# All queries, keys and values projected in the state space stage and kept as rows in DRAM, on one Trainium2 core

## Chip, cores, metric

One core of one Trainium2 chip runs the whole program. The metric is the device time of one execution in microseconds, as the median of three runs. PE is the matrix engine (TensorE), PEld its weight loads, DVE, ACT and POOL the vector, scalar and GpSimd engines, SP the engine that issues most DMAs.

## What is computed

One hybrid decoder layer on a sequence of 1024 positions, width 1024, float32:

```python
xn = rmsnorm(x, norm1_g)
q, k, v, u = split(xn @ w_in)              # 512 columns each; 8 heads of 64 for q, k, v
q, k = rmsnorm(q, q_norm_g), rmsnorm(k, k_norm_g)          # per head
attn = dilated_attention(q, k, v)          # causal, windows 128/512/2048, dilations 1/4/16, merged
ssm = s5_mixer(u, ...)                     # diagonal complex scan, gelu, then gated: z * sigmoid(z @ glu_w + b)
mix = concat(rmsnorm(attn), rmsnorm(ssm))
x = x + mix @ w_out
return x + square(relu(rmsnorm(x, norm2_g) @ w_mlp_up)) @ w_mlp_down
```

## The kernel before

Every large product is done in three passes (`mm3`: high by high, high by low, low by high), with both operands split into a high and a low part by one ACT and one DVE instruction (`split`, `split_scaled`; a weight is split when it is loaded, by `load_w`). The program runs through five stages.

**x and u.** `first_x(t)` loads tile t of the transposed input (128 positions), splits it, writes it to DRAM (`d_x`), takes its mean square (ACT squares; three halving additions, on DVE for even t and on POOL for odd t; one PE product `psn` with a column of ones) and projects the 512 columns of u (`psu`, 24 matmuls of 512 columns). The splits of odd tiles are on POOL.

**State space.** `ssm_tables`, `u_turn` and `ssm_main` make, for four groups of channels, tables (`ec`, `bj`, `bt`), input products (`psb`), a scan (`bw`, the state `X`), output products (`psy`) and the gelu; the last step transposes z (`pszt`) and writes `d_hz`. One of the four complex table products (`ec<-apow`) and two of the four multiplications that form X are on POOL. A written string of steps (u, T, B, t, m, p) sets the order; a "p" advances the projection of the first pair of heads.

**Attention.** Heads are handled in four pairs. `qkv(p)` projects the 384 columns of q, k, v of pair p, tile by tile (`psq`, 24 matmuls of 384 columns for each of 8 tiles): it reads the split x back through the POOL queue (`xt<-d_x`, 1 MB), norms q and k (four ACT squares with a sum, three POOL instructions, one DVE multiply, one ACT copy), transposes them (`pst`) into Qd and K2, and writes V2. `attn(p)` forms scores (`pss`, L541), masks and takes the minimum on DVE (L543), exponentials on ACT (L546), scales on POOL (L549), transposes (`psp`, L564), splits, and weighs the values (`pso`, L575). `weave(a, b, na, nb)` emits two generators in turn so that their shares advance evenly: attn(0), attn(1), attn(2) each beside the projection of the next pair, attn(3) beside `glu` (the gated unit) and `out_ssm` (the state space half of the output product, first 512 columns only).

**Output product.** For each of 8 tiles `out_tile` adds three parts (`out_part`, 12 matmuls each: state space half of columns 512 to 1023, attention half of both column halves), norms and transposes the result, and `operands` makes seven split operands for the last stage, three of them with POOL.

**MLP.** `up_proj` and `down_proj`, block products of 512 columns; not touched.

Tiles of the same place wait for each other: raw loads have two buffers (`rawp`), split weights five (`wp`), PSUM banks `mm` two, `tr` two, `s` three. The framework's scheduler moves instructions a little within an engine; each engine and each DMA queue then runs its own list strictly in order.

Of the kernel before, what the change touches and what calls it, by code (L numbers as in the profile page):

```python
# [8 lines left out]
F32 = mybir.dt.float32  # L9
# [25 lines left out]
def hybrid_layer_kernel(ctx: ExitStack, tc: tile.TileContext, io: dict, out: bass.AP):  # L35
# [27 lines left out]
    d_x = [dram.tile([128, 2, 8, 128], F32, name=f"d_x{t}") for t in range(8)]  # L63
# [34 lines left out]

    def load_rows(name, src, c, gains):

        return [load_w(f"{name}{i}", src[:, 2 * i:2 * i + 2, :], 2, c, gains, 2 * i) for i in range(4)]
# [54 lines left out]
    def kv_tiles(p):  # L156
        k, v, q0, q1 = (6, 7, 8, 9) if p % 2 else (2, 3, 4, 5)
# [3 lines left out]
    wu, kept = [], {}  # L161
    SQ = 170
    XS = 170
    XN = 128
    CA = 1

    def first_x(t):
# [3 lines left out]
        xt = place((2, 3, 4, 5, 2, 3, 0, 1)[t], [128, 2, 1024], F32R, "xt")  # L171
        split(xt[:, 0], xt[:, 1], raw, POOL if XS >> t & 1 else DVE)
# [6 lines left out]
        POOL.dma_start(out=d_x[t].rearrange("p a k m -> p a (k m)"), in_=xt.bitcast(F32))  # L179
        sq = sp2.tile([128, 1024], F32, tag="D", name="sq")  # L180
        if XN >> t & 1:
            nc.sync.dma_start(out=sq, in_=io["x"][t * 128:(t + 1) * 128, :])
            ms = sp2.tile([128, 1], F32, tag="ms", name="ms")
            ACT.activation(sq, sq, AF.Square, accum_out=ms)
        else:
            ACT.activation(sq, raw, AF.Square)
            for n in (512, 256, 128):
                (POOL if SQ >> t & 1 else DVE).tensor_tensor(sq[:, :n], sq[:, :n], sq[:, n:2 * n], op=OP.add)
        if not XN >> t & 1:
            pn = tr_bank("psn")  # L190
            PE.matmul(pn[:, 0:1], lhsT=sq[:, :128], rhs=ones, start=True, stop=True)
            ms = sp2.tile([128, 1], F32, tag="ms", name="ms")
            DVE.tensor_copy(ms, pn[:, 0:1])
# [4 lines left out]
        xv = xt.rearrange("p a (k m) -> p a k m", k=8)  # L198
        for k in range(8):
            mm3(ps, xv[:, 0, k], xv[:, 1, k], wu[k // 2][:, 0, k % 2], wu[k // 2][:, 1, k % 2], k == 0, k == 7)  # L200
        us = sp2.tile([128, 512], F32, tag="qkv_t", name="us")
        ACT.activation(us, ps, AF.Copy, scale=r)
        nc.scalar.dma_start(out=d_u[t * 128:(t + 1) * 128, :], in_=us)
        if t > 5:
            kept[t] = xt
# [122 lines left out]
    def ssm_tables(q):  # L328
# [22 lines left out]
        cmul(POOL if CA else DVE, ca[:, 0], ca[:, 1], a_r, a_i, c_r, c_ni, v1, v2, conj=True)  # L351
# [8 lines left out]
        bt = sp.tile([128, 2, 4, 128], F32, tag="bt", name="bt", bufs=3)  # L360
# [28 lines left out]
    def ssm_main(q, u, Et, ca, bt):  # L389
# [34 lines left out]
        POOL.tensor_tensor(v2, e_i, w_i, op=OP.mult)  # L424
# [3 lines left out]
        POOL.tensor_tensor(v2, e_i, w_r, op=OP.mult)  # L428
# [37 lines left out]
    def qkv(p, small, res):  # L466
        w = load_rows(f"wq{p}_", io["w_qkv"][p], 384, g1)
        K2, Qd, V2 = kv_tiles(p)
        res.update(K2=K2, Qd=Qd, V2=V2)

        def turn(t, qd):
            pt = tr_bank("pst").rearrange("p (h m) -> p h m", h=4)
            for h in range(4):
                PE.transpose(pt[:, h], qd[:, h].rearrange("p a e -> p (a e)"), ident)
            tt = slice(t * 128, (t + 1) * 128)
            split_scaled(Qd[0][:, :, tt], Qd[1][:, :, tt], pt[:, 0:2], gqk[:, 0:1])
            ACT.activation(K2[:, :, tt], pt[:, 2:4], AF.Copy, scale=gqk[:, 1:2])
            DVE.scalar_tensor_tensor(K2[64:128, :, tt], pt[64:128, 2:4], gqk[64:128, 1:2],
                                     K2[64:128, :, tt].bitcast(F32), op0=OP.mult, op1=OP.subtract)
# [611 lines left out]
```

## Time and profile before

| | |
|---|---|
| median of 3 runs | 1213.45 us (1211.04 to 1215.29) |
| the profiled execution | 1220.95 us, of which span 1219.2 us |
[...]
| PE busy | 1139.4 us (93%) |
| DVE busy | 841.0 us (69%) |
| ACT busy, POOL busy | 598.6 us (49%), 354.8 us (29%) |

The span is the time from the first to the last instruction of the profiled execution. A share of busy time is a mean over the five stages; the rows below give it by stage.

### The profile page before, as it was taken

The numbers are of one execution on the slowest core, as the hardware profiler recorded it, in microseconds if no ns is written. First come the engines' busy times: TensorE is split into PE (matmuls) and PEld (weight loads), VectorE is DVE, ScalarE is ACT, GpSimd is POOL, SyncE is SP. The second block draws the span as 40 slices with busy tenths as digits, with TensorE's granted clock in tenths as the row PEclk, the third lists the DMA queues.
The fourth block names the chain that finished last, engine by engine and source line by source line (L and its number), as shares of the span: only waits on it lengthen the run. The fifth ranks groups of instructions, "written<-read, shape, count | busy, mean of one in ns | idle before, by whom it ended". The sixth has DMA issues, their size and how long they took to land.

```text
span 1219.2 us, 16630 instructions
## 1 busy us (share of the span) xinstructions
PE 1139.4 (93%) x5734; PEld 956.7 (78%) x5734; DVE 841.0 (69%) x1557; ACT 598.6 (49%) x1276; POOL 354.8 (29%) x528
## 2 busy tenths in 40 slices
PE   6766989999999999999999999999999999999998
PEld 4554777888898877787777888888878888888887
DVE  7999785567676777666876566665656775576763
ACT  5222233677776786533555555555544333333332
POOL 6685642354545445313312111122110000000000
PEclk9886887899999999999999999999999999999999
DMA  7734432635355425753244434434379999575930
GB/s 288 272 115 106 151 112 70 211 114 178 129 155 170 143 96 166 243 191 121 75 159 173 167 145 165 145 140 167 144 294 398 387 387 352 193 240 183 333 140 35
DMA packets 101093, 227.15 MB, mean 186 GB/s; under 512 B 8848, under 2 KB 27792, under 8 KB 96144
## 3 DMA queue, kind: packets, MB, share of 16 engines
q1 hardware_dynamic: 85136, 154.13, 37.2%
q0 software_dynamic: 14432, 69.22, 15.7%
q10 hardware_dynamic: 1440, 2.73, 0.6%
q8 instruction: 45, 0.74, 0.3%
q14 instruction: 40, 0.33, 0.1%
HBM read 168.93 MB, written 57.11 MB: 185 GB/s over the span
## 4 chain that ended last, share of the span: by engine, by line
PE 70%; DVE 11%; DMA 6%; issue 5%; POOL 4%; ACT 4%; SPq 0%; ACTq 0%; DVEq 0%; POOLq 0%
PE psx L105 7%; PE psx L106 7%; PE psx L107 7%; PE psy L105 7%; PE psy L106 7%; PE psy L107 7%; PE pso L575 3%; PE psq L107 2%; PE psq L105 2%; PE psq L106 2%; PE pss L541 2%; PE psp L564 2%; PE psy L438 1%; PE pso L107 1%; PE pso L105 1%
## 5 line engine op out<-in xcount | busy, mean ns | idle before, releaser
L77 ACT ACTIVATE ud<-raw 128x1024 fp32r<-128x1024 f32 x112 | 112.9, 1053 | 184.8 <-PE psy L107 81.0
L78 DVE TENSOR_TENSOR ud<-raw,ud 128x1024 fp32r<-128x1024 f32 x112 | 132.6, 1221 | 83.6 <-ACT ud L77 83.6
L105 PE MATMUL psx<-X,wu 128*128 128x512 f32 (+1 forms) x260 | 101.1, 389 | 4.5 <-ACT st L871 3.2
L106 PE MATMUL psx<-X,wu 128*128 128x512 f32 (+1 forms) x260 | 100.4, 386 | 0.7 <-DVE X L78 0.7
L107 PE MATMUL psx<-X,wu 128*128 128x512 f32 (+1 forms) x260 | 100.5, 386 | 0.5 <-DVE wu L78 0.5
L105 PE MATMUL psy<-ud 128*128 128x512 f32 x256 | 99.6, 389 | 0.0
L106 PE MATMUL psy<-ud 128*128 128x512 f32 x256 | 99.6, 389 | 0.0
L107 PE MATMUL psy<-ud 128*128 128x512 f32 x256 | 99.6, 389 | 0.0
L78 DVE TENSOR_TENSOR wu<-wm,wu 128x512 fp32r<-128x512 f32 x112 | 75.5, 701 | 30.8 <-ACT wu L77 30.6
L105 PE MATMUL psq<-wq,xt 128*128 128x384 f32 x256 | 93.7, 366 | 0.9 <-DMA xt<-d_x 0.8
L77 ACT ACTIVATE wu<-wm 128x512 fp32r<-128x512 f32 x112 | 66.7, 625 | 53.1 <-DMA wm<-in_w_up_dram 27.0
L106 PE MATMUL psq<-wq,xt 128*128 128x384 f32 x256 | 90.6, 354 | 0.5 <-DVE wq L82 0.5
L107 PE MATMUL psq<-wq,xt 128*128 128x384 f32 x256 | 90.8, 355 | 0.0
L875 POOL DMA_DIRECT2D d_a<-st x80 | 43.5, 544 | 130.1 <-DVE st L884 65.9
L106 PE MATMUL psx<-ud 128*128 128x512 f32 x192 | 74.8, 390 | 0.0
L105 PE MATMUL psx<-ud 128*128 128x512 f32 x192 | 74.7, 389 | 0.0
L107 PE MATMUL psx<-ud 128*128 128x512 f32 x192 | 74.7, 389 | 0.0
L980 DVE TENSOR_TENSOR raw<-raw 128x1024 f32<-128x1024 f32 x40 | 49.7, 1249 | 28.7 <-DMA raw<-in_w_down_dram 28.7
L549 POOL TENSOR_SCALAR s<-s,dn 128x128 f32<-128x128 f32 (+3 forms) x64 | 50.2, 787 | 47.9 <-DVE dn L548 45.9
L78 DVE TENSOR_TENSOR pt<-psp,pt 128x128 fp32r<-128x128 f32 (+2 forms) x96 | 51.1, 552 | 15.9 <-ACT pt L77 15.2
L105 PEld LDWEIGHTS psx<-X,wu 128*128 128x128 f32 x260 | 48.8, 188 | 16.5 <-ACT st L871 4.6
L575 PE MATMUL pso<-pt,V 128*128 128x256 f32 x320 | 54.6, 294 | 3.5 <-ACT pt L77 1.9
(294 smaller groups left out, 3012.5 us busy)
## 6 DMA issues: line engine op xcount, KB each, us to landing
raw<-in_w_down_dram SPq DMA_DIRECT2D x96, 512.0 KB, 9.0
xt<-d_x POOLq DMA_DIRECT2D x30, 1024.0 KB, 5.2
raw<-d_a SPq DMA_DIRECT2D x56, 512.0 KB, 8.1
d_a<-st POOLq DMA_DIRECT2D x80, 256.0 KB, 2.6
wm<-in_w_up_dram SPq DMA_DIRECT2D x32, 512.0 KB, 3.7
d_x<-xt POOLq DMA_DIRECT2D x8, 1024.0 KB, 5.1
d_a<-o POOLq DMA_DIRECT2D x32, 256.0 KB, 2.8
wq_r<-in_w_qkv_dram SPq DMA_DIRECT2D x16, 384.0 KB, 3.9
```

Of the source, the lines that this page charges most:

```text
L77: ACT.activation(h, src, AF.Copy)
L78: eng.tensor_tensor(l, src, h.bitcast(F32), op=OP.subtract)
L105: PE.matmul(ps, lhsT=ah, rhs=bh, start=start, stop=False, skip_group_check=more)
L106: PE.matmul(ps, lhsT=ah, rhs=bl, start=False, stop=False, skip_group_check=more)
L107: PE.matmul(ps, lhsT=al, rhs=bh, start=False, stop=stop, skip_group_check=more)
L438: PE.matmul(psy[s][:, a], lhsT=X[s * 64:s * 64 + 64, ri, a, :], rhs=ca[s * 64:s * 64 + 64, ri, a].rearrange("p d c -> p (d c)"), start=Fal ...
L541: PE.matmul(ps[:, :cw], lhsT=Qd[a][:, h, b * 128:(b + 1) * 128], rhs=K2[:, h, c0:c0 + cw], start=a == 0, stop=a == 1)
L549: POOL.tensor_scalar(s[:, :n], s[:, :n], dn, 1.0, op0=OP.mult, op1=OP.mult)
L564: PE.transpose(ps[:, kb * 128:(kb + 1) * 128], P[j][:, (k0 + kb) * 128:(k0 + kb + 1) * 128], ident)
L575: PE.matmul(po[:, :256], lhsT=V2[:, k0 + kb, h, :], rhs=pt[:, a, kb, :], start=k0 + kb == 0 and a == 0, stop=k0 + kb == nb - 1 and a == 1)
L875: POOL.dma_start(out=d_a[blk // 2][i][blk % 2], in_=st)
L980: DVE.tensor_tensor(rb, rb, raw_unit(wd(n, *b1)), op=op)
```

## The change

The projection of q, k and v no longer goes by pairs of heads. `project(c)` projects all 512 columns of q (c=0), k (c=1) or v (c=2), 24 matmuls of 512 columns for each of 8 tiles, all in the state space stage; two "p" are one tile. The split x of all tiles stays in SBUF (six places and the two U buffers), so only four tiles are written to `d_x` and read back. q and k are normed there (one ACT square, one DVE reduction, three POOL instructions, one DVE multiply, one POOL copy) and written to DRAM as rows `d_q`, `d_k`; v goes to `d_v`. `heads(p)` later reads the rows of a pair, transposes them four tiles at a time and makes Qd, K2 and V2. The weave partners of the four attentions are now the heads of the next pair and pieces of `glu` and `out_ssm`; `out_ssm` does both column halves, so that `out_tile` has two parts instead of three. The sums for the norms of x, attn and ssm become 8 or 4 PE products with ones instead of additions on DVE or POOL. Everything that `first_x`, `ssm_tables`, `ssm_main` and `operands` gave to POOL as a two-input operation goes to DVE.

```diff
+    ORDER = ((6, 7, 0, 1, 2, 3, 4, 5), (4, 5, 0, 1, 2, 3, 6, 7), (2, 3, 0, 1, 6, 7, 4, 5))
+    BACK = {(1, 6): 4, (1, 7): 5, (2, 4): 2, (2, 5): 3}
-            for n in (512, 256, 128):
-                (POOL if SQ >> t & 1 else DVE).tensor_tensor(sq[:, :n], sq[:, :n], sq[:, n:2 * n], op=OP.add)
...
+        for k in range(8):
+            PE.matmul(pn[:, 0:1], lhsT=sq[:, k * 128:k * 128 + 128], rhs=ones, start=k == 0, stop=k == 7)
...
+    def project(c):
+        w = [load_w(f"wq{c}_{i}", io["w_qkv"][c, :, 2 * i:2 * i + 2, :], 2, 512, g1, 2 * i) for i in range(4)]
+        for t in ORDER[c]:
+            if (c, t) in BACK:
+                res[t] = place(BACK[c, t], [128, 2, 1024], F32R, "xt")
+                POOL.dma_start(out=res[t], in_=d_x[t])
+            ps = mm_bank("psq")
+            x_mm(ps, res[t], w, range(4))
+            yield
+            x_mm(ps, res[t], w, range(4, 8))
+            if c < 2:
+                row = sp2.tile([128, 8, 2, 64], F32, tag="rows", name="rows")
+                sq = row[:, :, 1]
+                ACT.activation(sq, ps.rearrange("p (h e) -> p h e", e=64), AF.Square)
+                f = sp2.tile([128, 8], F32, tag="f", name="f")
+                DVE.tensor_reduce(f, sq, axis=AX.X, op=OP.add)
+                rsqrt(f, f, r2[:, t:t + 1], 8)
+                POOL.tensor_scalar(f, f, rstd1[:, t:t + 1], 1.0, op0=OP.mult, op1=OP.mult)
+                DVE.tensor_tensor(row[:, :, 0], ps.rearrange("p (h e) -> p h e", e=64),
+                                  f[:, :, None].to_broadcast([128, 8, 64]), op=OP.mult)
+                POOL.tensor_scalar(row[:, :, 1], row[:, :, 0], 1.0, 1.0, op0=OP.mult, op1=OP.mult)
...
+            nc.sync.dma_start(out=d_qkv[c][t * 128:(t + 1) * 128, :], in_=row)
...
-        cmul(POOL if CA else DVE, ca[:, 0], ca[:, 1], a_r, a_i, c_r, c_ni, v1, v2, conj=True)
+        cmul(DVE, ca[:, 0], ca[:, 1], a_r, a_i, c_r, c_ni, v1, v2, conj=True)
...
-        POOL.tensor_tensor(v2, e_i, w_r, op=OP.mult)
+        DVE.tensor_tensor(v2, e_i, w_r, op=OP.mult)
...
+    def heads(p, out_):
+        K2, Qd, V2 = kv_tiles(p)
...
+            for c in range(2):
+                st = rawp.tile([128, 1024], F32, tag="raw", name="qk_r").rearrange("p (t h e) -> p t h e", t=4, h=2)
+                rows(c, 4 * hf, 4, st.rearrange("p t h e -> p t (h e)"), 256)
+                for h in range(2):
+                    pt = tr_bank("pst")
+                    for t in range(4):
+                        PE.transpose(pt[:, t * 128:t * 128 + 128], st[:, t, h], ident)
+                    if c == 0:
+                        split_scaled(Qd[0][:, h, tt], Qd[1][:, h, tt], pt, gqk[:, 0:1])
...
-    weave(attn(3, **prev), tail(), 24.5, 43.0)
+    weave(attn(0, **cur[0]), chain(heads(1, cur[1]), some(g, 5)), 24.5, 17.0)
+    weave(attn(1, **cur[1]), chain(heads(2, cur[2]), g, some(o, 2)), 24.5, 17.0)
+    weave(attn(2, **cur[2]), chain(heads(3, cur[3]), some(o, 6)), 24.5, 19.7)
+    weave(attn(3, **cur[3]), o, 24.5, 21.6)
```

Where the instructions stand now, at three places. First PE at the end of the state space stage, before: the last transposes of z (`pszt`) stand among scores of attn(0) (`pss`) and the projection of the second pair (`psq`).

```order
L541 MATMUL pss<-K_944,Qd 128x256 x4
L105 MATMUL psq<-wq_0_2040,xt 128x384
L106 MATMUL psq<-wq_0_2040,xt 128x384
L461 MATMUL pszt<-pack,z_1867 128x128 x8
L107 MATMUL psq<-wq_0_2040,xt 128x384
L105 MATMUL psq<-wq_0_2040,xt 128x384
L474 MATMUL pst<-pack,qd 128x128 x4
```

Now 228 of the 576 `psq` stand behind the last `pszt`, and behind the last of them the transposes of rows (`pst`) and the scores follow directly:

```order
L103 MATMUL psq<-wq_3_2263,xt 128x512
L104 MATMUL psq<-wq_3_2263,xt 128x512
L506 MATMUL pst<-pack,qk_r 128x128 x8
L542 MATMUL pss<-K_2423,Qd 128x256 x6
L506 MATMUL pst<-pack,qk_r 128x128 x12
L542 MATMUL pss<-K_2423,Qd 128x256 x2
L542 MATMUL pss<-K_2423,Qd 128x384 x2
```

So no projection is left beside the first scores. Second, SP at the same place, before: the mask (`bias`) is loaded between weight loads of the second pair.

```order
L463 DMA d_hz<-hz 128x1024
L91 DMA wq_1_r<-in_w_qkv_dram 128x768
L671 DMA bias<-in_bias_dram 128x1024
L91 DMA wq_2_r<-in_w_qkv_dram 128x768
```

Now the mask stands behind the read-back of v, whose second half waits for the last row of v:

```order
L229 DMA d_v<-row 128x512
L496 DMA v_r<-d_v 128x4x128
L496 DMA qk_r<-d_q 128x4x256
L496 DMA v_r<-d_v 128x4x128
L672 DMA bias<-in_bias_dram 128x1024
```

The load of the mask has moved behind a wait for the end of the projections. Third, DVE in a scan of the state space stage, before (the two products that form `s_1581` and `s_1586` are on POOL):

```order
L417 SCALAR_TENSOR_TENSOR bw<-rho,bw 128x128 x7
L423 TENSOR_TENSOR s_1580<-ec,bw 128x4x127
L427 TENSOR_TENSOR s_1585<-ec,bw 128x4x127
L425 TENSOR_TENSOR X<-s_1580,s_1581 128x4x127
L429 TENSOR_TENSOR X<-s_1585,s_1586 128x4x127
```

Now, with those two products on DVE and the norm of a projected tile (`f`, `rows`) between:

```order
L442 SCALAR_TENSOR_TENSOR bw<-rho,bw 128x128 x7
L448 TENSOR_TENSOR s_1402<-ec,bw 128x4x127
L449 TENSOR_TENSOR s_1403<-ec,bw 128x4x127
L452 TENSOR_TENSOR s_1407<-ec,bw 128x4x127
L450 TENSOR_TENSOR X<-s_1402,s_1403 128x4x127
L453 TENSOR_TENSOR s_1408<-ec,bw 128x4x127
L219 TENSOR_REDUCE f<-rows 128x8
L454 TENSOR_TENSOR X<-s_1407,s_1408 128x4x127
L222 TENSOR_TENSOR rows<-psq,f 128x8x64
```

Two products have moved to DVE and two instructions of the projection have joined the chain.

## Rows read from the trace of the kernel before

**Rows 1.** Stages: window, length; busy PE, PEld, DVE, ACT, POOL; clock, DMA share, GB/s.

```profile
0.00:79.00 79.00, 54.99 (x215) 43.16 (x215) 67.80 (x223) 30.05 (x39) 53.23 (x61) 0.92 0.66 240
79.00:226.00 147.00, 119.14 (x770) 100.36 (x771) 111.17 (x195) 47.07 (x139) 74.53 (x91) 0.76 0.38 113
226.00:515.00 289.00, 273.97 (x1683) 244.06 (x1681) 206.50 (x560) 205.87 (x626) 138.15 (x230) 1.00 0.49 161
515.00:597.00 82.00, 78.78 (x362) 64.80 (x361) 55.23 (x81) 33.79 (x72) 23.68 (x33) 0.94 0.45 148
597.00:1219.20 622.20, 612.49 (x2707) 504.35 (x2707) 400.34 (x502) 281.83 (x404) 65.25 (x116) 1.00 0.60 214
```

**Rows 2.** The same windows for tile psq: PE, PEld, DVE, ACT.

```profile
79.00:226.00 147.00, 48.02 (x198) 40.53 (x199) 5.39 (x15) 10.00 (x71) 0.76 0.38 113
226.00:515.00 289.00, 120.80 (x567) 95.60 (x565) 19.14 (x50) 31.66 (x217) 1.00 0.49 161
```

**Rows 3.** Timeline of PE near 266 us: start, duration, instruction.

```profile
265.80 0.33 PE L105 MATMUL psq<-wq,xt 128*128 128x384 f32 x1
265.97 0.33 PE L106 MATMUL psq<-wq,xt 128*128 128x384 f32 x1
```

**Rows 4.** Timeline of PE near 800 us.

```profile
800.50 0.39 PE L105 MATMUL psy<-X,wu 128*128 128x512 f32 x1
800.73 0.39 PE L106 MATMUL psy<-X,wu 128*128 128x512 f32 x1
```

**Rows 5.** Tile psn: instructions, duration min/median/max.

```profile
L520 PE MATMUL psn<-ones,ssq x32: 164/250/352, 461.4 to 558.3; 128*128 128x1 f32 x32
```

**Rows 6.** Timeline of DVE, 102 to 111 us.

```profile
102.04 1.58 DVE L115 TENSOR_TENSOR s<-eh,el 128x512 f32<-128x512 f32 x1
...
109.94 0.68 DVE L114 TENSOR_TENSOR s<-rpow,bb 128x512 f32<-128x512 f32 x1
110.54 0.68 DVE L115 TENSOR_TENSOR s<-rpow,bb 128x512 f32<-128x512 f32 x1
```

**Rows 7.** Timeline of POOL at 103 us.

```profile
103.04 1.54 POOL L115 TENSOR_TENSOR s<-apow,pack 128x512 f32<-128x512 f32 x1
```

**Rows 8.** Groups of DVE by line and shape, 226 to 515 us: busy, mean ns.

```profile
L82 DVE SCALAR_TENSOR_TENSOR wq<-wq_r,pack,wq 128x384 fp32r<-128x384 f32 x18 | 10.6, 614 | 3.6 <-ACT wq L81 3.6
L748 DVE SCALAR_TENSOR_TENSOR x<-pso,rsm,x 128x512 f32<-128x512 f32 x8 | 6.0, 746 | 2.1 <-DMA x<-in_x_dram 2.1
```

**Rows 9.** The stretch 226 to 515 for tile pst: PE, PEld, DVE, ACT.

```profile
226.00:515.00 289.00, 15.57 (x100) 11.36 (x100) 24.82 (x52) 24.11 (x51) 1.00 0.49 161
```

**Rows 10.** The same stretch for attention's lines L541, L564, L575: PE, PEld.

```profile
226.00:515.00 289.00, 47.63 (x188) 30.54 (x188) 1.00 0.49 161
...
226.00:515.00 289.00, 45.39 (x288) 34.00 (x288) 1.00 0.49 161
...
226.00:515.00 289.00, 54.62 (x320) 44.80 (x320) 1.00 0.49 161
```

**Rows 11.** The chain that ended last, at two places: start, duration.

```profile
227.88 5.90 DMA bias<-in_bias_dram
...
268.56 0.87 PE psp L564 x8
```

**Rows 12.** DMA issues by line: size, median us to landing.

```profile
xt<-d_x POOLq DMA_DIRECT2D x30, 1024.0 KB, 5.2
...
d_x<-x SPq DMA_DIRECT2D x24, 256.0 KB, 2.4
```

**Rows 13.** Windows of all engines: two stretches of the state space stage.

```profile
104.00:122.00 18.00, 11.23 (x62) 9.14 (x62) 16.20 (x28) 2.83 (x6) 6.60 (x8) 0.53 0.20 36
200.00:221.00 21.00, 21.00 (x70) 17.11 (x70) 8.82 (x25) 8.34 (x18) 4.08 (x7) 0.51 0.16 54
```

**Rows 14.** Who waited for whom, 226 to 515 us: total, times, longest.

```profile
DVE pt L78 <- ACT pt L77: 15.2, 27, 2.0
```

**Rows 15.** Tile psu: ACT's copy of a tile, duration min/median/max.

```profile
L202 ACT ACTIVATE us<-psu,rstd x8: 667/684/690, 22.0 to 79.3; 128x512 f32<-128x512 f32 x8
```

More of the change, by code (lines that the diff above doesn't have):

```diff
@@ L170, in first_x @@
         nc.sync.dma_start(out=raw, in_=io["x_t"][t])
-        xt = place((2, 3, 4, 5, 2, 3, 0, 1)[t], [128, 2, 1024], F32R, "xt")
-        split(xt[:, 0], xt[:, 1], raw, POOL if XS >> t & 1 else DVE)
+        if t < 6:
+            xt = place(t, [128, 2, 1024], F32R, "xt")
+        else:
+            xt = sp.tile([128, 2, 1024], F32R, tag="U", name="xt", bufs=2)
+        split(xt[:, 0], xt[:, 1], raw)
         if not wu:
@@ L517, in mix_scale, with rows @@
-    def mix_scale(a, tiles):
-        for t in tiles:
-            pn = tr_bank("psn")
-            PE.matmul(pn[:, 0:1], lhsT=ssq[:, a, t * 128:(t + 1) * 128], rhs=ones, start=True, stop=True)
-            vs = part("vs", [128, 1], "vs")
-            DVE.tensor_copy(vs, pn[:, 0:1])
-            rsqrt(rsm[:, t, a:a + 1], vs, 1.0 / 512, 1)
+        out_.update(K2=K2, Qd=Qd, V2=V2)
+        def rows(c, t0, nt, to, w):
+            nc.sync.dma_start(out=to, in_=d_qkv[c][t0 * 128:(t0 + nt) * 128, w * p:w * p + w].rearrange("(t m) c -> m t c", m=128))
@@ L657, in hybrid_layer_kernel @@
             next(main[q], None)
-    assert next(proj, None) is None
+    for n, _ in enumerate(proj):
+        if n == 12:
+            first = heads(0, prev)
+        if n > 12:
+            next(first)
+    for _ in first:
+        pass
     ssm.close()
@@ L730, in operand, with load_mix @@
         return XC[i]
-    def mixed(t, a):
-        return [x[:, t // 2] for x in operand(MIX[t % 2, a])]
-    def load_mix(t, a):
-        mx = rawp.tile([128, 1024], F32, tag="raw", name="mx")[:, :512].rearrange("p (k m) -> p k m", k=4)
-        nc.sync.dma_start(out=mx, in_=d_mix[a][:, :, t * 128:(t + 1) * 128].rearrange("k p m -> p k m"))
-        split(*mixed(t, a), mx)
+    def load_mix(t, a, where):
+        mx = rawp.tile([128, 1024], F32, tag="raw", name="mx")
+        mv, sq = [mx[:, i * 512:i * 512 + 512].rearrange("p (k m) -> p k m", k=4) for i in range(2)]
+        nc.sync.dma_start(out=mv, in_=d_mix[a][:, :, t * 128:(t + 1) * 128].rearrange("k p m -> p k m"))
+        mt = place_turn(where, [128, 2, 4, 128], F32R, "mt")
+        split(mt[:, 0], mt[:, 1], mv)
+        ACT.activation(sq, mv, AF.Square)
+        pn = tr_bank("psn")
+        for k in range(4):
+            PE.matmul(pn[:, 0:1], lhsT=sq[:, k], rhs=ones, start=k == 0, stop=k == 3)
+        vs = part("vs", [128, 1], "vs")
+        DVE.tensor_copy(vs, pn[:, 0:1])
+        rsqrt(rsm[:, t, a:a + 1], vs, 1.0 / 512, 1)
+        return mt
@@ new lines, in some @@
+    def some(gen, n):
+        for _ in range(n):
+            v = next(gen, None)
+            if v is None:
+                return
+            yield v
+    cur = [prev, {}, {}, {}]
+    g, o = glu(), out_ssm()
+    weave(attn(0, **cur[0]), chain(heads(1, cur[1]), some(g, 5)), 24.5, 17.0)
+    weave(attn(1, **cur[1]), chain(heads(2, cur[2]), g, some(o, 2)), 24.5, 17.0)
+    weave(attn(2, **cur[2]), chain(heads(3, cur[3]), some(o, 6)), 24.5, 19.7)
+    weave(attn(3, **cur[3]), o, 24.5, 21.6)
```

216 lines of the change are left out of this document (74 added, 142 removed).

## The prediction, on record before the run

> **What bounds the kernel now.** Read first the windows by stage [rows 1]. In the MLP (622.2 us) PE is busy 612.5, and the change does not touch it. In the attention stage (289 us) PE is busy 274.0 at full clock, a share of 0.948, with DVE and ACT at 206 each: PE sets the pace. In the output product (82 us) PE has 78.8. The state space stage (147 us) is the loose one: PE 119.1 at a mean clock of 0.76, DVE 111.2; neither is full, and the chains between DVE, ACT, POOL and PE set the end. The first stage (79 us) has DVE at 67.8 and PE at 55.0. So the idle PE time is in the first 226 us, and PE work that leaves the attention stage is worth its full time.
>
> **The projections cost PE the same.** Two 384-column matmuls follow each other after 0.17 us [rows 3], two of 512 columns after 0.23 [rows 4]. Before: 768 x 0.174 = 134 us. After: 576 x 0.227 = 131 us. The change saves no projection; it moves it.
>
> **First stage.** 64 products with ones replace 7 single ones; each is two matmul rows, so 128 rows instead of 14. The trace has no long run of them: a lower bound is the 0.87 us for eight 128-column matmuls [rows 11], 0.11 a row, an upper one the median 0.25 [rows 5]; I take 0.11, as these also queue behind one another. That is +12 us of PE in a stage with 24 us of PE idle. DVE gains four splits of 1024 columns and loses twelve halving additions, which I take as nil. 79 stays 79; at worst the 12 us would lie on the path.
>
> **State space stage.** Without `psq` PE has 119.1 - 48.0 = 71 us there [rows 1, 2], 54 of it if the clock were full. All 131 us of projection now come in. By the order of PE 348 of the 576 `psq` (79 us) stand among the state space products and 228 (52 us) behind the last of them. DVE loses `psq` work (5.4) and most of its transposed splits and gains: 32 products from POOL at 0.60 from start to start [rows 6], 19 us; reduction and multiply of about 14 tiles, 28 x 0.6 = 17; six more weights split. Against that stands what POOL costs DVE now: with a two-input POOL product running (1.54 us) [rows 7] the same DVE product takes 1.58 instead of 0.68 [rows 6]. I estimate 15 such collisions (between none and all 32), which gives 13 us back. DVE: 111 - 11 + 19 + 17 + 4 - 13 = 127 us for the mixed part. PE has 133 to 150 there. Both stay under or at the 147 of before, so I take 150 for the mixed part, 52 for the rest at full clock and 3 for the 32 transposes of the first pair: 205, or **+58**. Bounds: +42 (PE never waits and always has full clock: 54 + 131 + 4 = 189) and +96 (all added projection, 131 - 35, serial to the 147).
>
> [...]
>
> Four tiles of x still come back through POOL, 5.2 us each [rows 12]. By the order each is issued at least two tiles (11 us) ahead of its matmuls, so they are hidden; without that cover they would cost up to 21. The rows written and read back are 21 MB in place of some 30 MB of x; the DMA share is 0.38 to 0.49 here [rows 1], no bound. The next matrix's weights are split while PE finishes the tile before, one of four ahead: at most 3 us each time, in the bounds.
>
> **Start of attention.** Before, the mask landed 5.9 us after its issue [rows 11] while PE had projections of the second pair. Now none is left, the mask's load stands on SP behind the read-back of v, and that waits for the last row of v. After the last `psq`: ACT's copy 0.7 [rows 15], the row's write 2.4 [rows 12], the mask 5.9: 9 us, less 1.5 of transposes and scores that PE can do. [...] I add 2.5 for some 5 us of attention's work at half clock: **+10** (bounds 3 and 18).
>
> **Attention.** Of the 567 `psq` that leave the stage, each frees 0.174: 98.7 us. In come 96 matmuls of the second column half of `out_ssm`, 21.8, and 36 rows of `psn`, 4. The transposes stay. PE: 274.0 - 98.7 + 21.8 + 4 = 201 us. DVE: 206.5 less `psq` work 19.1 [rows 2], less weights 10.6 [rows 8], and the Q and K splits fall from 24.8 (52 of 256 columns) [rows 9] to about 17 (24 of 512 at 0.7), with six for V at 0.7, +4, and eight more output additions at 0.75 [rows 8], +6: 179. ACT falls from 206 by at least 31.7 [rows 2], to under 175. POOL loses all norms and sums. PE still has the most to do, but 179 beside 201 is close, where it was 206 beside 274. With PE's share at 0.948 the stage would take 212; at 0.92, which I take since the partners are thinner, 201 / 0.92 = 219: **-70**. Bounds: 212 (-77) and, at a share of 0.79, 254 (-35).
>
> **Output product.** 96 matmuls leave (21.8 us), 59 rows of `psn` come (6.5): PE 78.8 - 15.3 = 63.5, and at 0.91 of the time 70: **-12**. DVE keeps 55 (eight additions less, twelve subtractions from POOL more), a share of 0.79, so it can take back some: bounds -5 and -17.
>
> **Sum.** 58 + 10 - 70 - 12 = **-14**: a span of 1205 instead of 1219.2. The profiled execution took 1220.95, 7.5 above the median; taken from the median 1213.45, the change gives **1199**.
>
> **Rivals.**
> *Attention runs at the pace of its own chain (slower).* In that chain scores go PE, DVE, ACT, DVE, POOL, PE, ACT, DVE, PE. Its own matmuls are 47.6 + 45.4 + 54.6 = 148 us [rows 10]; beside them PE had 126 us of other work to fill waits, and will have 53. Its waits are there now: DVE stands 15.2 us for ACT's half of the split [rows 14], with all that other work beside it; the masking of the next scores is queued behind it on DVE, and PE's next transposes wait for the bank. At a PE share of 0.79 the stage takes 254 and the median comes to 1234. It decides below 0.86: 79 + 205 + 10 + 201 / 0.86 + 70 + 622 = 1219. Against it: at 219 us DVE's share is 0.82 and ACT's under 0.80.
> *The state space stage stretches.* PE is in order, and a projection that waits for a bank (two `mm` banks, shared with `psb`; a bank is free only after ACT, DVE, three POOL instructions and DVE again) holds back the products of the scan. At +85 instead of +58 the median is 1226. For it: PE was at half clock for much of that stage; against it: projections are ready work, and more of it keeps the clock up.
> *Denser.* If every one of the 32 moved products cost DVE a 0.9 us wait before, the mixed part gives back 29 instead of 13, PE alone bounds it, and the stage comes to +45; with the start at +4, attention at its old share (-77) and the output at -15 that is -43, median 1170.
> *Nothing.* The time only moves: attention at 0.87 gives 1212.
>
> **Chances.** Forecast (1183 to 1208) 0.41; denser 0.11; nothing 0.13; attention's chain 0.22; stretched stage 0.13. A change below 0.3% (1210 to 1217) can hardly be told from none here. Faster: 0.41 + 0.11 = 0.52; same 0.13; slower 0.22 + 0.13 = 0.35. The range of 8 in 10 takes in half of the denser case and of both slower ones: 1172 to 1240; the forecast's own is 1183 to 1208.
>
> **What would show it.** Right: the last `pszt` near 229 us, the last `psq` near 281; a PE gap of 6 to 9 us before the first L543 score instruction, ended by the mask; the last `pso<-pt,V` near 514 with PE at 0.9 or more; output product about 70 us; MLP unchanged at 622. DVE's 512-wide products at 0.68 throughout would show the collisions gone. Wrong: `psq` that waits for DVE's multiply (bank), long DVE idle in attention ended by ACT together with PE below 0.86, or a DVE share above 0.9 in either stage.

## The result, and the profile after

The changed kernel takes **1253.41 us** (median of four runs, 1251.47 to 1257.78) against 1213.45: a ratio of **1.034** (95% interval 1.030 to 1.037). It is 40 us slower; the forecast was 1199, 14 us faster, with a range of 1172 to 1240. The profiled execution took 1253.21 us, its span 1251.4.

The windows of the changed kernel by stage, columns as in [rows 1] (first stage; the part where projections stand among the state space products; the tail of projections alone; the start of attention; attention; output product; MLP):

```profile
0.00:75.00 75.00, 65.86 (x375) 55.83 (x376) 55.36 (x228) 33.08 (x42) 31.03 (x41) 1.00 0.59 205
75.00:247.00 172.00, 139.04 (x834) 109.19 (x833) 111.52 (x218) 36.79 (x58) 60.27 (x83) 0.87 0.34 110
247.00:308.00 61.00, 58.23 (x258) 47.35 (x257) 11.54 (x16) 15.46 (x22) 10.12 (x16) 0.94 0.47 156
308.00:326.00 18.00, 10.36 (x53) 8.50 (x51) 9.21 (x27) 9.67 (x23) 2.44 (x6) 0.72 0.72 233
326.00:563.00 237.00, 210.40 (x1208) 173.37 (x1208) 178.19 (x454) 148.79 (x317) 64.28 (x104) 0.94 0.36 116
563.00:632.00 69.00, 61.26 (x324) 49.91 (x323) 50.08 (x85) 34.52 (x76) 15.80 (x32) 0.99 0.53 175
632.00:1251.40 619.40, 611.78 (x2712) 505.81 (x2710) 400.44 (x506) 282.25 (x405) 60.56 (x112) 1.00 0.60 214
```

Beside the stages of [rows 1] and the forecast for each:

| stage | before | forecast | after | miss |
|---|---|---|---|---|
| first | 79 | 79 | 75 | -4 |
| state space, all projections | 147 | 205 | 233 | +28 |
| start of attention and attention | 289 | 229 | 255 | +26 |
| output product | 82 | 70 | 69 | -1 |
| MLP | 622.2 | 622.2 | 619.4 | -3 |

Together the miss is 46 us of span. The other 8 of the 54 are the step from the profiled execution to the median: 7.5 us were taken off because the profiled execution before was that far above its median. After, profiled time and median agree.

So two stages went wrong, by nearly the same amount. Look first at the state space stage. In its mixed part neither PE (139 of 172 us) nor DVE (111.5) is full. Who waited for whom there, the first rows for DVE in 75 to 247 us (total, times, longest), then the first for PE in 75 to 308 us:

```profile
DVE rows L222 <- POOL f L221: 28.8, 13, 4.1
DVE f L219 <- ACT rows L217: 10.1, 6, 2.9
...
PE psb L424 <- DVE rows L222: 17.9, 5, 5.0
```

And one such wait in the timeline of PE, ACT, DVE and POOL near 100 us (in square brackets the idle time before, and what ended it):

```profile
98.81 0.39 PE L104 MATMUL psq<-wq,xt 128*128 128x512 f32 x1
...
99.24 0.60 ACT L217 ACTIVATE rows<-psq 128x512 f32<-128x512 f32 x1 [4.50 <-PE psq L104]
...
99.86 0.69 DVE L219 TENSOR_REDUCE f<-rows 128x8 f32<-128x512 f32 x1 [2.90 <-ACT rows L217]
...
100.65 0.27 POOL L74 TENSOR_SCALAR rsq<-f,r 128x8 f32<-128x8 f32 x1 [4.20 <-DVE f L219]
101.01 1.65 POOL L75 TENSOR_TENSOR f<-rsq,mhalf 128x8 f32<-128x8 f32 x1
102.76 0.28 POOL L221 TENSOR_SCALAR f<-f,rstd 128x8 f32<-128x8 f32 x1
...
103.08 0.69 DVE L222 TENSOR_TENSOR rows<-psq,f 128x512 f32<-128x512 f32 x1 [2.53 <-POOL f L221]
...
103.83 1.55 PE L424 MATMUL psb<-U,bt 128*64 128x128 f32 x12 [4.62 <-DVE rows L222]
```

Read it from the bottom: PE's next work, `psb` of the scan, wants an `mm` bank. That bank holds a projected tile until its norm is through: ACT's square, DVE's sum, three POOL instructions, DVE's multiply, 4.5 us from 99.24 to 103.77. Meanwhile DVE does nothing else either: it stands 2.53 us for POOL's factor, and with that the scan behind it in DVE's list. (The trace has DVE's instructions of a scan in the order of the list shown with the change: the scan at 203 us goes from L448 at 203.25 us over the reduction, L219, at 206.23 and L454 at 206.82 to the multiply, L222, at 209.80, with 2.30 us of waiting for POOL before it and nothing between.)

In attention, the first waits of PE (326 to 563 us), and three windows around the longest (the first two overlap):

```profile
PE pso L102 <- ACT mt L78: 6.1, 1, 6.1
PE pso L576 <- ACT pt L78: 5.5, 7, 2.8
```

```profile
399.00:419.00 20.00, 16.43 (x95) 12.66 (x93) 19.12 (x56) 16.53 (x34) 7.73 (x9) 1.00 0.36 126
405.00:425.00 20.00, 10.84 (x59) 7.69 (x57) 17.05 (x42) 13.28 (x27) 8.13 (x8) 0.85 0.39 127
425.00:445.00 20.00, 19.74 (x108) 16.91 (x107) 9.49 (x26) 7.46 (x20) 3.47 (x10) 0.81 0.24 79
```

PE stands for one instruction 6.1 us, up to 424.6; the window behind it is 99% busy at a mean granted clock of 0.81. In the 20 us up to the wait DVE is busy 19.1, so it is nearly full there. Before, the whole attention stage ran at 1.00 [rows 1].

### The profile page after: what moved, and what is told of

Read it like the earlier page. It is cut to its first block, busy times and chain, and to the rows that moved or that the text cites. A ratio compares the mean times of both kernels' runs of the same rounds, so it can differ in the third digit from the quotient of the medians.

```text
span 1251.4 us, 16189 instructions
## 1 busy us (share of the span) xinstructions
PE 1156.9 (92%) x5752; PEld 950.0 (76%) x5752; DVE 816.3 (65%) x1530; ACT 560.6 (45%) x939; POOL 244.5 (20%) x391
## 4 chain that ended last, share of the span: by engine, by line
PE 62%; DMA 6%; DVE 5%; ACT 4%; issue 1%; POOL 0%; SPq 0%; ACTq 0%; DVEq 0%
PE psx L102 7%; PE psx L104 7%; PE psx L103 7%; PE psy L102 7%; PE psy L104 7%; PE psy L103 7%; PE pso L576 3%; PE psp L565 2%; PE pss L542 2%; PE pso L102 2%; DMA wm<-in_w_up_dram 2%; PE pso L103 2%; PE pso L104 2%; PE psn L726 1%; PE psq L102 1%; PE psq L103 1%
## 5 line engine op out<-in xcount | busy, mean ns | idle before, releaser
L102 PE MATMUL psq<-wq,xt 128*128 128x512 f32 x192 | 82.3, 431 | 10.8 <-DVE s L437 4.8
L103 PE MATMUL psq<-wq,xt 128*128 128x512 f32 x192 | 80.0, 417 | 0.0
L104 PE MATMUL psq<-wq,xt 128*128 128x512 f32 x192 | 79.5, 415 | 0.0
L576 PE MATMUL pso<-pt,V 128*128 128x256 f32 x320 | 58.7, 308 | 7.1 <-ACT pt L78 5.5
L102 PE MATMUL pso<-wo,mt 128*128 128x512 f32 x128 | 53.9, 422 | 6.6 <-ACT mt L78 6.1
L576 PEld LDWEIGHTS pso<-pt,V 128*128 128x128 f32 x320 | 46.9, 198 | 17.1 <-ACT pt L78 12.1
```

Of the source, the lines that this page charges most:

```text
L102: PE.matmul(ps, lhsT=ah, rhs=bh, start=start, stop=False, skip_group_check=more)
L103: PE.matmul(ps, lhsT=ah, rhs=bl, start=False, stop=False, skip_group_check=more)
L104: PE.matmul(ps, lhsT=al, rhs=bh, start=False, stop=stop, skip_group_check=more)
L576: PE.matmul(po[:, :256], lhsT=V2[:, k0 + kb, h, :], rhs=pt[:, a, kb, :], start=k0 + kb == 0 and a == 0, stop=k0 + kb == nb - 1 and a == 1)
```

## The experiments

Three theories for the state space stage. *Bank*: the norm holds the `mm` banks, and `psb` waits for them. *List*: DVE waits inside the norm for ACT and POOL, and what stands behind it in DVE's list is late. *Work*: PE simply has more to do there, part of it at the lower clock. For attention: *mask*, *weights*, and *chain* (attention's own chain sets the pace, as the slower rival had it). In all diffs the base is the changed kernel unless said otherwise; ratios are against the kernel before, run beside them on the same chip.

**The scan's products on banks of their own** (`e1_psb_own`).

```
-        psb = [mm_bank(f"psb{ri}")...
+        psb = [s_bank(f"psb{ri}")...
```

> The two psb banks of the scan come from the three s banks; the two mm banks serve the projections alone. Bank theory (a projection's bank is held until ACT, DVE, POOL and DVE are through with its norm, and the psb products behind it in PE's order wait for it): the psb waits for DVE's rows (17.9 us in the changed kernel) vanish, the last psq falls from 307.5 to 287 to 294 us, median 1234 to 1240. List theory (DVE works in order, and it is its own waits for ACT and POOL inside the norm, 39 us, that delay the scan, whoever holds a bank): the psb waits for rows go, but reappear behind other DVE work; last psq at 303 or later, median 1249 to 1255. Work theory (PE has simply more to do there, part of it at half clock): no change, 1251 to 1256.

Measured: 1237.98 us, ratio 1.019 (1.017 to 1.021). The last `psq` ends at 292 us in place of 308, and no `psb` waits for `rows` any more. That the bank cost some 15 us is shown (18 by the ratios). But `psq` now waits for `rows` itself, 9.8 us in six waits: the projections meet their own banks.

**No norm** (`e2_no_norm`).

```
-                ACT.activation(sq, ps..., AF.Square)
-                DVE.tensor_reduce(f, sq, ...)   (and rsqrt, and POOL's product with rstd1)
-                DVE.tensor_tensor(row[:, :, 0], ps..., f..., op=OP.mult)
+                ACT.activation(row[:, :, 0], ps..., AF.Copy, scale=rstd1[:, t:t + 1])
```

> Leaves the norm of queries and keys out: their rows are one ACT copy scaled as v's are, and POOL's doubling; DVE's reduction, three POOL instructions and DVE's multiply are gone (the output is not the layer's). Bank and list theories alike: the state space stage loses its stretch, last psq 280 to 290 us (forecast of before was 281), median 1226 to 1236. If e1 moves little and this much, it is DVE's list and not the bank. Work theory: under 6 us, 1247 to 1254.

Measured: 1211.12 us, ratio 0.997 (0.995 to 0.999). More than any theory gave: the last `psq` is at 267 us, 41 earlier, and the stage is 14 us *under* the forecast's 281. Everything that the stage lost, and more, hangs on the norm of the projected tiles, its waits and its 20 us of work on DVE together; work theory falls, since PE has the same products to do.

**The multiply on POOL** (`e6_norm_on_pool`): ACT frees the bank, DVE only sums.

```
+                ACT.activation(row[:, :, 0], ps..., AF.Copy)
-                DVE.tensor_tensor(row[:, :, 0], ps..., f..., op=OP.mult)
+                POOL.tensor_tensor(row[:, :, 0], row[:, :, 0], f..., op=OP.mult)
```

> ACT copies the projected tile out of its bank right after its square; DVE only reduces; POOL, which makes the factor, also multiplies (in SBUF). Nothing is left out. So the bank is freed by ACT as with banks of their own (there 15 us), and DVE no longer waits for POOL's factor (28.8 us in 13 waits). List theory (after the banks the rest of the 41 us that leaving the norm out gave is DVE's in-order wait for POOL): last psq at 270 to 283 us, median 1214 to 1227. Bank theory alone: as with separate banks, last psq near 292, median 1235 to 1240. A loss against that if POOL's two-input products of 1.5 us hold DVE up 16 times, up to 14 us.

Measured: 1228.73 us, ratio 1.012 (1.008 to 1.016), last `psq` at 284, just outside the 270 to 283 of the list theory: 24 us of 41 are back, 8 more than by banks alone. This edit frees the banks of the projections earlier and spares DVE its wait for the factor, so it does not say which of the two gave the 8. The rest moved: POOL is busy 97 us of the 172 from 75 to 247 us (60 in the changed kernel), and other work on DVE waits for it and for ACT (75 to 300 us):

```profile
DVE ga L472 <- POOL ga L471: 14.2, 3, 5.8
DVE f L220 <- ACT rows L217: 12.8, 6, 5.0
```

**Values first** (`e10_v_first`): the same work in another order. The read-back and the splits of a pair's values also move ahead of its queries and keys.

```
-    def project(c):
+    def project(j):
+        c = (2, 0, 1)[j]
```

> The three projections come in the order values, queries, keys (the heads of a pair read values first too). The same work, but eight of the some fourteen tiles among the state space products are now values, which need no norm, and the eight keys with their norm stand in the tail, where DVE has nothing else. Norm theory (each normed tile among the state space products costs about 41/14.5, near 3 us, by its bank and by DVE's waits): the mixed part is 20 to 26 us shorter, the tail stays at 55 to 62 us, and V is there early, so that attention's start gives 2 to 6 us more unless the last keys' norm takes that back: median 1222 to 1236. Work theory (it is the amount of work in the stage): 1250 to 1256.

Measured: 1229.7 us, ratio 1.011 (1.009 to 1.013). From the last `psu` to the last `pszt` it takes 153 us in place of 178, the tail 59 in place of 60: the norm costs where it stands among the scan, and next to nothing where DVE has no other work. But attention's start did not gain: PE stands 10 us there now, for the keys' norm and their way through DRAM.

**POOL's products given back** (`e7_pool_back`).

```
-        cmul(DVE, ca[:, 0], ca[:, 1], ...)
+        cmul(POOL, ca[:, 0], ca[:, 1], ...)
-        DVE.tensor_tensor(v2, e_i, w_i, op=OP.mult)    (and e_i, w_r)
+        POOL.tensor_tensor(v2, e_i, w_i, op=OP.mult)
```

> Undoes one part: the ca table's cmul and two products of each state step go back to POOL. Collision theory of the prediction (a POOL product makes DVE's last 1.58 in place of 0.68 us; moving 32 products cost DVE 19 us and gave back 13): DVE's share falls by 19 and its products lengthen, the stage moves by -6 to +8 us, median 1247 to 1261. If DVE's load were what stretched the stage: -15, median 1238.

Measured: 1267.64 us, ratio 1.043 (1.040 to 1.046): 12 us slower than the changed kernel (the ratios' difference, 0.96%), beyond both expectations. So this part of the change *helped*. One group of DVE in that kernel and, below, in the changed one (75 us to about the last `pszt`):

```profile
L450 DVE TENSOR_TENSOR X<-s,s 128x508 f32<-128x508 f32 x4 | 7.0, 1758 | 4.7 <-POOL s L449 4.7
```

```profile
L450 DVE TENSOR_TENSOR X<-s,s 128x508 f32<-128x508 f32 x4 | 2.7, 677 | 0.0
```

`X` is a link of the scan's chain: with POOL's half it waits 1.2 us and then takes 1.76 in place of 0.68, in each of four steps. What the table adds to the 12 us is not told apart in this kernel.

**The same part alone, in the kernel before** (`e12_before_dve`; `CA = 1` becomes `CA = 0`, and the two state products as above, POOL to DVE).

> One part alone, in the kernel before: the ca table and the two products of each state step move from POOL to DVE, everything else stays. Collision theory of the prediction (19 us more DVE work, 13 given back, neither on the path): -4 to +6 us against the kernel before. Queue theory (in the changed kernel giving them back to POOL cost 12 us because the norm's factors stood behind POOL's long products; before, few normed tiles stand among the state space products): also near nothing here, -5 to +3. A gain of 8 or more would say that the change carried a part that helps by itself.

Measured: 1205.25 us, ratio 0.991 (0.989 to 0.994): **10 us faster than the kernel before**, and the lowest median of all (the interval of `e13_start` below overlaps with it). Neither theory had it. DVE's busy time did not grow by the move. The busy times of the whole run, in this kernel, then in the changed kernel and in `e7_pool_back`:

```profile
PE 1127.6 (94%) x5734; PEld 947.1 (79%) x5734; DVE 833.6 (69%) x1589; ACT 598.6 (50%) x1276; POOL 319.9 (27%) x496
```

```profile
PE 1156.9 (92%) x5752; PEld 950.0 (76%) x5752; DVE 816.3 (65%) x1530; ACT 560.6 (45%) x939; POOL 244.5 (20%) x391
```

```profile
PE 1161.1 (92%) x5752; PEld 954.9 (75%) x5752; DVE 816.1 (64%) x1498; ACT 560.9 (44%) x939; POOL 284.6 (22%) x423
```

With 32 products more DVE is busy 7 us less than in the kernel before (841.0), and in the changed kernel as long as without them: its other products are that much shorter when POOL's long ones are gone (`s<-eh,el` on one line 1.64 us in `e7_pool_back`, 0.68 in the changed kernel).

**Half of that part** (`e14_before_state`): in the kernel before, the two state products alone.

> In the kernel before, only the two products of each state step move from POOL to DVE; the ca table stays on POOL. Wait theory (in the kernel before PE waits 5.8 us for X and DVE 4.7 us for POOL's half of it; the gain of 10 us with both moved is this wait in the chain of the scan): most of it, -6 to -11 us against the kernel before, 1204 to 1209. Table theory (the gain is in the tables: PE stands 4.5 us for kp and DVE's other products are slowed beside POOL's long ones): -4 to +1, 1211 to 1216.

Measured: 1209.65 us, ratio 0.995 (0.994 to 0.997): 5.7 us of the 10, just short of the 6 to 11 of the wait theory. In the kernel before, the group of `X` on DVE and that of POOL's product ahead of it:

```profile
L425 DVE TENSOR_TENSOR X<-s,s 128x508 f32<-128x508 f32 x4 | 7.0, 1738 | 4.7 <-POOL s L424 4.7
...
L424 POOL TENSOR_TENSOR s<-ec,bw 128x508 f32<-128x508 f32 x4 | 8.9, 2219 | 29.2 <-DVE bw L417 29.2
```

The first `X` there, and POOL's product beside it (timeline):

```profile
120.96 1.25 POOL L428 TENSOR_TENSOR s<-ec,bw 128x508 f32<-128x508 f32 x1
121.03 1.73 DVE L425 TENSOR_TENSOR X<-s,s 128x508 f32<-128x508 f32 x1 [1.16 <-POOL s L424]
```

And PE's waits for `X` and for the table's `kp` (75 to 230 us):

```profile
PE psy L438 <- DVE X L425: 5.8, 2, 2.9
PE psbt L364 <- DVE kp L385: 4.5, 1, 4.5
```

`X` first waits for POOL's product of 2.22 us, which it reads, and then runs beside POOL's next one. PE's waits for `X` fall from 5.8 us to 1.8 here and to 1.1 in `e12_before_dve`. The other half is put down to the table by difference: PE's 4.5 us for `kp` are still 3.9 here and gone with the table on DVE too. The two intervals touch, so the split is rough.

**The mask** from ACT's queue, ahead of the V splits (`e3_mask_early`), and from POOL's, before the last projections end (`e9_mask_pool`).

```
-    nc.sync.dma_start(out=bias, in_=io["bias"])
+    nc.scalar.dma_start(out=bias, ...)      (e9: POOL.dma_start)
+    for _ in first:                         (this loop stood ahead of the mask)
+        pass
```

> The mask's load is issued from ACT's queue ahead of the V splits of the first pair, in place of SP's queue behind the read-back of v. Mask theory (9 us from the last psq to the first score operation, the mask last): the first L544 operation comes 4 to 8 us earlier, the wait for bias goes, median 1245 to 1250. Rival (V's rows and splits end at 317 us, 2 us before the mask lands, and are late next; the clock stays at half all the same): 1251 to 1254.

> The mask's load is issued from POOL's queue, some 20 us before the last projection ends, so that it is there when the first scores are. Mask theory: the first L544 operation follows the first scores within 2 us, near 312 in place of 319 us; median 1245 to 1249. Rival, as seen when ACT issued it (V's rows, and the read-back of the second pair's first rows, which PE meets 7.4 us before the second block of scores, are late next): first pso at 321 or later, median 1250 to 1255.

Measured: 1255.19 and 1255.21 us, ratio 1.033 both times (1.031 to 1.035, 1.030 to 1.036). No gain. But the first edit hardly moved the mask: ACT issues it at 312.8 us, behind its copies, where SP had issued it at 313.2, and DVE still stands for it. It is no test of the mask. The second is: issued at 280.6, the mask lands 6.8 us later, DVE does not wait for it, and the first score operation comes 7.5 us after the start of the last `psq` in place of 11.8. The time did not follow, so there the rival held. The first score operation in the first and in the second of these kernels, each with PE's wait next to it:

```profile
319.31 0.29 DVE L544 CUSTOM_DVE_ANT_0 s<-pss,bias 128x128 f32<-128x128 f32 x1 [2.72 <-DMA bias<-in_bias_dram]
320.16 1.30 PE L506 MATMUL pst<-pack,qk_r 128*128 128x128 f32 x5 [7.39 <-DMA qk_r<-d_q]
```

```profile
321.93 0.29 DVE L544 CUSTOM_DVE_ANT_0 s<-pss,bias 128x128 f32<-128x128 f32 x1
322.04 1.51 PE L506 MATMUL pst<-pack,qk_r 128*128 128x128 f32 x6 [4.44 <-DVE V L522]
```

With the mask there, the read-back of the last projected rows is late: V's split waits for it on ACT and DVE, and the rows of the next pair (`qk_r`), which PE transposes next, are asked for only at 317.6 us. Which of the two ends PE's 4.44 us is open: V's split ends 0.14 us before them.

**The output weights.** The two half tiles of the state space output product that stand behind the gated unit go behind the next heads (`e4_out_later`); the same, but with their four weights still issued early (`e8_wo_ahead`).

```
 (e4)  attn(1): heads(2), g, some(o, 2)  ->  heads(2), g
       attn(2): heads(3), some(o, 6)     ->  heads(3), some(o, 8)
 (e8)  attn(1): heads(2), g, some(o, 1)      attn(2): heads(3), some(o, 8)
         w = [load_wo(ch, 1) for ch in range(2)]
+        yield 0.1
```

> The gated unit's part in the second pair's attention stays, but the two half tiles of the state space output product that stood right behind it move to the third pair's attention, behind the heads of the fourth pair. Handoff theory (PE stands 6.1 us at 424 us for the first mixed tile, which is written by the gated unit's last step and read back, and the clock is at its lower level for 24 us between 419 and 467): the 6.1 us wait and the half clock there go, attention ends 9 to 15 us earlier, median 1238 to 1245. Chain theory (attention's own chain sets the pace and PE waits somewhere anyway): under 4 us, 1249 to 1255.

> The four output weights of the state space half are still issued behind the gated unit in the second pair's attention, but the first tile's products only come after the heads of the fourth pair. Weight theory (the 6.1 us at 424 us, and 14.1 us at 457 us when only the order was changed, are PE waiting while four weights come through two raw buffers and five weight slots): the wait falls under 2 us, the half clock behind it (24 us) goes, median 1238 to 1247. Handoff theory (it is the gated unit's rows that are late, or attention's own chain): 1250 to 1259.

Measured: `e4_out_later` 1258.87 us, ratio 1.037 (1.034 to 1.040), a miss: the wait grew to 14.1 us. `e8_wo_ahead` 1248.61 us, 1.028 (1.024 to 1.032), 5 to 7 us better than the changed kernel, by the medians or by the ratios, whose intervals just overlap (1.030 to 1.037 there); just short of its expectation. PE's wait for the first mixed tile in the two:

```profile
PE pso L102 <- ACT mt L78: 14.1, 1, 14.1
```

```profile
PE pso L102 <- ACT mt L78: 3.2, 1, 3.2
```

In the first of them ACT splits the weights one by one as they come through the two `raw` buffers, and the first mixed tile is behind them (timeline of ACT):

```profile
454.17 1.33 ACT L82 ACTIVATE wo<-wo_r,pack 128x512 fp32r<-128x512 f32 x2 [1.43 <-DMA wo_r<-in_w_o_dram]
456.33 0.63 ACT L78 ACTIVATE mt<-mx 128x512 fp32r<-128x512 f32 x1 [0.82 <-DMA mx<-d_mix]
```

In the changed kernel itself SP shows the same order: the last write of the gated unit's rows at 411.83 us, and the read of the first mixed tile only behind the last weight.

```profile
411.83 0.33 SPq L696 DMA_DIRECT2D d_mix<-ga  x1
...
418.76 0.33 SPq L92 DMA_DIRECT2D wo_r<-in_w_o_dram  x1
420.90 0.37 SPq L720 DMA_DIRECT2D mx<-d_mix  x1
```

So it is the weights, and not the gated unit's rows: the second column half brought four weights to a place where two had been.

**All mendings together** (`e11_all`: values first, banks, weights, mask from POOL, the first pair's last transposes woven into its attention), and the same with the second pair's first transposes ahead of the first pair's last keys (`e13_start`; its edit is shown against `e11_all`).

```
-    weave(attn(0, **cur[0]), chain(first, heads(1, cur[1]), some(g, 5)), ...)
+    weave(attn(0, **cur[0]), chain(some(h1, 5), first, h1, some(g, 5)), ...)
```

> Values first, the scan's psb products on banks of their own, the output weights of the state space half one pair ahead, the mask from POOL's queue, and the last transposes of the first pair woven into its attention. Norm theory: with banks of their own the six normed tiles left among the state space products cost less still; with the 7 us of the weights and some of the start the median comes to 1203 to 1220, level with or under the kernel before. If the gains overlap (DVE's list is then set by the scan itself): 1220 to 1232.

> As the kernel with values first and all mendings, but the transposes of the second pair's values and first half (queries and keys) stand ahead of those of the first pair's last keys, which wait for the norm, the write and the read-back of the last projected tile (11.1 us of PE at 283 us, and 17 us at the lower clock behind it). Round-trip theory: the wait falls under 4 us, median 1196 to 1204 (against 1210.7). Rival (attention's first blocks have no more work to give and the wait only moves to the scores or to the first pso): 1207 to 1214.

Measured: 1210.7 us, ratio 0.996 (0.995 to 0.998), and 1207.18 us, 0.993 (0.991 to 0.995). The first is as expected. The second comes to its rival's edge: PE's wait at the start goes from 11.1 to 7.1 us and no further, since the second pair's own rows are read late. The intervals of the two kernels overlap, so the 3.5 us between them are not clear of noise. In both kernels, PE's first wait in 265 to 300 us:

```profile
PE pst L519 <- DMA qk_r<-d_k: 11.1, 1, 11.1
```

```profile
PE pst L519 <- DMA qk_r<-d_q: 7.1, 1, 7.1
```

The state space stage over eight of these kernels, worked out from their traces (us; from the last `psu` to the last `psq`; idle is what PE was not busy, low clock the time at the lower of the two granted levels, 0.50 and 1.00 in the changed kernel's trace):

| kernel | stage | PE busy | idle | low clock |
|---|---|---|---|---|
| `e7_pool_back` | 250 | 202 | 48 | 55 |
| changed kernel | 238 | 203 | 36 | 51 |
| `e1_psb_own` | 223 | 197 | 26 | 31 |
| `e6_norm_on_pool` | 214 | 190 | 23 | 17 |
| `e10_v_first` | 212 | 191 | 20 | 21 |
| `e13_start` | 198 | 189 | 10 | 14 |
| `e11_all` | 197 | 187 | 10 | 10 |
| `e2_no_norm` | 196 | 186 | 10 | 7 |

Low clock falls with the idle time, though not in step. The last three rows are near what PE's work alone takes.

## Why the prediction was wrong, point by point

**The projections cost PE the same: right.** In the kernels with the fewest waits the stage takes 196 to 198 us with PE busy 186 to 189, close to the lower bound of 189.

**First stage: right** within what it varies by (75 against 79; the last `psu` starts at 71.9 us before, and between 69.2 and 74.0 in the changed kernel and its variants). The 64 `psn` products are not to be seen in the time.

**State space stage, +58: this step failed**, at +86. Its work was even overestimated: DVE has 111.5 us in the mixed part, not 127. The false step is "Both stay under or at the 147 of before, so I take 150": the stage was priced as the larger of two sums, though the profile of before already showed neither engine full. What sets it is the way of each projected tile through four engines, 4.5 us, with a bank held and DVE's list stopped; before, the short projections of one pair among the scan had little of that (DVE's multiply waited 1.2 us for POOL's factor, after, 28.8); after, fourteen tiles have it. The slower rival *state space stage stretches* named this mechanism, the banks and the chain, and its +85 is the measured size; it got a chance of 0.13 because "projections are ready work". They are ready for PE; their ends are not ready for DVE. Shown: 15 us by the banks alone, 41 by the whole norm, 26 by the order alone. How the rest beyond the banks divides between DVE's list and the projections' own banks was not separated.

**POOL's products: the mechanism right, its size too small, and so the sign of the price wrong.** DVE's products of the scan run at 0.68 us, as forecast (0.677 above), and most of the tables' too. The move was costed at 19 more and 13 back, a loss of 6 us on DVE. Measured, DVE loses nothing: by the forecast's own 19, 26 us came back in the kernel before (841.0 to 833.6) and 19 in the changed one (816.1 and 816.3). So 15 collisions were too few, and the premise of the rival *denser*, 29 back, was nearer, though its stage was not. The time fell by 10 us in the kernel before and by 12 in the changed one. Four of the slowed products (`X`, 1.74 us and 1.2 of wait) lie in the scan's chain, where PE waits at the end; the sum of DVE's time has no term for that.

How long one such product takes is seen in the timeline of the kernel before, above: `X` starts 0.07 us behind POOL's product of 1.25 us and takes 1.73, where the same line takes 0.68 with both products on DVE (`e12_before_dve`). That is 1.05 us more, and 1.18 us of POOL's product were left when it started. What makes it so long no run shows.

**Start of attention, +10: the size right, the reason wrong.** PE does 10.4 us of work in the 18 us, 5.8 of it at a granted clock of 0.50 (313.3 to 323.6 us): 7.6 us idle and, as an estimate, half of the 5.8, 2.9, lost to the clock. The forecast's 2.5 us for work at half clock were the author's estimate, which no run shows as a term of its own: before, the granted clock was 0.53 and 0.51 in two stretches of the state space stage, the second of them full of PE's work [rows 13], and these 2.9 us are what the changed kernel showed in its place. The first score operation comes at 319.4, 11.8 us after the start of the last `psq` at 307.5. PE's longer wait, and the end of it on DVE in the changed kernel, V's last split and the first score operation:

```profile
315.80 1.94 PE L506 MATMUL pst<-pack,qk_r 128*128 128x128 f32 x8 [4.92 <-DMA qk_r<-d_q]
...
317.13 0.69 DVE L522 TENSOR_TENSOR V<-v_r,V 128x512 fp32r<-128x512 f32 x1 [2.14 <-ACT V L521]
...
319.38 0.29 DVE L544 CUSTOM_DVE_ANT_0 s<-pss,bias 128x128 f32<-128x128 f32 x1 [0.77 <-DMA bias<-in_bias_dram]
```

The mask ends 0.77 us of wait, but the round trip of the last projected rows (copy, write, read, split) ends only 1.6 us before it, PE's longest gap is a wait for rows and not for the mask, and with the mask out of the way (`e9_mask_pool`) nothing was gained. The forecast priced the transfer that ended last and not the one right behind.

**Attention, 219: this step failed too**, by all of the 26 us of start and attention. Of the 255 us from 308 to 563 the start's own loss is 10.5, so attention has 244.5. In it PE's work comes to about 207 us at full clock against the 201 forecast (an estimate: 220.8 busy, less half of the 27.4 that lay at the lower clock, granted 0.50); the `psn` products alone took 9.2 where 4 were forecast. PE is idle 27 us against 18, and the lower clock costs 11 us (half of 21.6 busy) against none. So the term that was put at nothing without a reason is the clock: 201 / 0.92 takes the full clock of before for granted, and from 326 to 563 27 us were at the lower level. The share is 0.89 by busy time and 0.84 as work at full clock, not 0.92.

PE's waits of over 1 us in that window come to 13.3 us, and nearly half of them is the weights' 6.1; `e8_wo_ahead` halved that wait and gained 5 to 7 of the 26 us. What the rest hangs on is open. The rival *attention runs at the pace of its own chain* was to decide below a share of 0.86 and would have made long DVE waits for ACT; DVE's waits for `pt` fell from 15.2 [rows 14] to 5.7 us, so its named sign did not come, though its sum (1234) lies nearer and PE itself still waits 5.5 us for ACT's `pt`. A full DVE, as in the 20 us ahead of the weights' wait, is another candidate. Neither this nor the remaining waits of 1 to 3 us were tried.

**Output product and MLP: right** (69 for 70; 619 for 622).

**From profile to median: failed by 7.5 us.** One execution's distance from its median is not a property of the next kernel.

## What to carry to other kernels

Filling a loose stage with work of another engine is priced by the longest path of one new unit through *all* engines, and by what it holds on the way (a bank, a place in an in-order list), not by comparing sums of busy time alone; here neither engine was full before, and the sums were not the bound after. Put the units without a long tail (here values, which need no norm) among the tight chain and those with one where the other engines are free: that alone was worth 24 us, or 28 by the ratios. And run each part of a large change alone: one small part was worth 10 us by itself, and the large rearrangement, with the mendings that were put together, came to 0.993 (0.991 to 0.995), no better than that part alone, 0.991 (0.989 to 0.994).

## What the runs showed of the hardware

POOL's power with exponent -0.5 on a handful of numbers is the longest link of the norm (1.65 of 4.5 us), and it grows with the columns. Groups of POOL in the changed kernel (the last is a power with other exponents) and, below, in the kernel before:

```profile
L75 POOL TENSOR_TENSOR f<-rsq,mhalf 128x8 f32<-128x8 f32 x16 | 26.8, 1673 | 1.1
L75 POOL TENSOR_TENSOR rsm<-rsq,mhalf 128x1 f32<-128x1 f32 x16 | 9.5, 593 | 1.2
...
L259 POOL TENSOR_TENSOR dt<-ebase,pack 128x16 f32<-128x16 f32 x1 | 3.1, 3061 | 6.6 <-DMA pack<-in_pack_dram 6.6
```

```profile
L74 POOL TENSOR_TENSOR f<-rsq,mhalf 128x4 f32<-128x4 f32 x8 | 9.3, 1160 | 0.4
```

0.59 us for one column, 1.67 for eight, 3.06 for sixteen: from these three, as an estimate, about 0.16 us a column. Before, four factors took 1.16 us; with eight a tile the change made the longest link longer, though there are fewer of them.

Behind the 6.1 us wait in attention, two products of 512 columns follow each other after 0.43 us, in place of the 0.23 of [rows 4]:

```profile
429.12 0.63 PE L102 MATMUL pso<-wo,mt 128*128 128x512 f32 x1
429.55 0.63 PE L103 MATMUL pso<-wo,mt 128*128 128x512 f32 x1
```

The granted clock there is 0.50, from 419.1 to 432.8 us, and it is so again for 10 us by 467; from 425 to 445 PE was busy 19.7 of 20 us. From 405 to 418.5 the granted clock was 1.00, and PE was busy 10.4 of these 13.5 us; the clock fell 0.6 us into the wait, which began at 418.5. It rose 8 us after PE's work began again: 424.6 to 432.8 us is full of products at 0.50, and 432.8 to 440 at 1.00. So, as an estimate, half of these 8.2 us, 4.1, was lost beside the wait's own 6.1. What brings the clock down and up again is not shown here.
